# Trunk of mixed attention layers on one core: weight tiles seven and five, squares by pairs, rotary steps on VectorE, retention scores a unit later

## The chip, the cores and the metric

The kernel runs on one core of a Trainium2 chip. A core has TensorE (called PE in the profile; it multiplies matrices and loads its weights beside the multiplication, PEld), VectorE (DVE), ScalarE (ACT), GpSimd (POOL) and SyncE (SP), which issues most DMA transfers here. The engines run side by side and wait for one another through semaphores; each executes its own instructions in the order in which the program lists them. The metric is the time of one execution on the device in microseconds, the median over the runs; lower is better. One execution was also taken by the hardware profiler.

## The reference

The model is a decoder trunk of two layers on 256 tokens of width 1024, in float32, followed by a last RMSNorm. A layer is:

```python
for l in range(DEPTH):                      # DEPTH = 2
    h = rms_norm(x, attn_norm[l])
    p = h @ w_in[l]                         # 6560 columns
    cq, ckv, k_rope, mq, mk, mv, rq, rk, rv, rg, g_mla, g_moba, g_ret = split(p)
    o_mla  = causal attention over low-rank cq, ckv (normed, projected up) with rotary parts
    o_moba = block attention over mq, mk, mv; with 256 tokens one block: causal attention, partial rotary
    o_ret  = retention over rq, rk, rv in chunks of 128 with decay, group norm, times silu(rg)
    merged = sigmoid(g_mla) * (o_mla @ w_mla) + sigmoid(g_moba) * (o_moba @ w_moba) + sigmoid(g_ret) * (o_ret @ w_ret)
    x = x + merged @ w_out[l]
    h = rms_norm(x, mlp_norm[l])
    x = x + square(relu(h @ w_mlp_up[l])) @ w_mlp_down[l]
return rms_norm(x, final_norm)
```

Rotary embedding turns pairs of rows of a head: `x1*cos - x2*sin` and `x1*sin + x2*cos`. RMSNorm needs, for each token, the sum of the squares of its 1024 values.

## The kernel before

**Precision.** Products run as three TensorE products of split numbers: a value is held as a high part and a low part in a fast 32-bit format, and `high*high + low*high + high*low` is summed in PSUM (`three`, L221 to L223). In a turned projection (`project_turned`) the same three go as eight products over both parts of the activations (L378, 512 columns) and eight with the low part of the weights (L380, 256 columns).

**Weights.** All weights stream from memory once. A block of 128 x 1024 values is loaded by SP into a tile `raw` (`transfer`, a pool of RAW = 7 tiles); ScalarE copies it into its high part `whi` (L200), and VectorE subtracts to get its low part `wlo` (L202). There are six tiles of each; a block is loaded and split one unit ahead or more, and a tile comes free when the last matmul that reads it is done.

**Activations.** X holds the residual stream turned, 128 rows (channels) by 256 tokens in each of eight row chunks. `Normed` makes the operand of the products after a norm: for each chunk ScalarE writes the high part of x times the gain (L236) and VectorE the low part (L237), tiles `xs`. The factor 1/rms isn't in there; it is put in behind the products, from sums of squares that are made beside them. For that, `Normed.square(n)` (L266 to L273) squares a chunk on ScalarE (128x256) and adds it to `sqsum`; the addition runs on GpSimd or VectorE by the argument `on_pool`, and in this kernel on GpSimd. `Normed.stats` (L293) sums over the partitions with four small matmuls into `pss`, scales them on VectorE (L325), takes the power −1/2 on GpSimd (L326) and halves a copy on VectorE (L299). `stats_row` turns the result into a row by two transposes (L331), which ScalarE copies to `rrow` (L321). Layer 0's first norm takes its statistics from x by tokens instead and uses no `square`.

**Order of the work.** A layer is a list of units (`prog`): in layer 1 the low-rank projection b0, then mq (four units of turned projection), mk (four), mv, the gates gmla and gmoba of the branches, retention's rqk, rv and rg, the branch products, and so on; in layer 0 b0 and mq are made together in the start. Beside the units, steps are hung on places of the list by `at(slot(key, j), step)`: a step is emitted behind that unit. So `c_norms` (with squares and statistics in layer 1) follows unit 1 of mq, `stats_row` unit 2, `moba_rope` for mq follows the mk units 1 and 3 in layer 1, and for mk the units 1 and 3 of gmla0. The scores of retention (`ret_scores`, L444) follow unit 0 of rg. A scheduler that simulates the engines' times then fixes the order of each engine's instructions, over all that is emitted and with limits from the pools; a stretch at the layer change and the ends is in the written order on TensorE.

**Rotary of turned heads.** `project_turned` leaves pairs of heads in `qkraw` (L385 adds the two halves of an accumulator). `rope_turned` then loads a copy with the quarters swapped by four DMAs on SP (`qkoth`, L406), and makes `qkT = qkraw*cos + qkoth*sin` with one product L409, one product L410 and one sum L411, each over 128x512. For MoBA all three run on GpSimd, for retention L409 and L411 run on VectorE and L410 on GpSimd. The tables with cos and sin are multiplied by 1/rms on GpSimd (L397).

**Accumulators.** PSUM holds four accumulators `acc` of 512 columns and four for other uses. In layer 1, b0 holds two of `acc` until `c_norms` has read them.

The lines that the change touches are L196, L197 (the split tiles), L249 to L273 (`Normed`), L400 to L412 (`rope_turned`), L643 to L650 (`c_norms`), L720 to L723 (`moba_rope`), L823 (place of the mq rope), L887 (`ret_pair`), L998 (place of the scores) and L1219 (RAW).

## Time and profile before

| | |
|---|---|
| runs | 838.18, 837.26 and 837.96 us, median 837.96 |
| profiled execution | 838.08 us, of which 836.3 us span |
| TensorE clock granted | 0.998 in the mean |
| TensorE busy | 827.3 us, 99% of the span, 4382 instructions |
| VectorE busy | 587.7 us, 70% |
| ScalarE busy | 483.8 us, 58% |
| GpSimd busy | 92.7 us, 11%, 82 instructions |
| read from memory | 150.77 MB, 182 GB/s over the span |

The span runs from the first to the last instruction on the core; the time of an execution is 1.8 us longer. Rows of the profile name an engine, a line of the kernel, an operation and the tiles `out<-in`; a row of a timeline starts with its start and its length in us; rows of groups end with the summed busy time, the mean duration of one in ns, and the idle time ahead of them with what released it. The duration of a matmul in a row holds the latency of its pipeline: the next one starts well before it ends, 0.23 us after it for 512 columns, 0.12 us for 256.

### The profile page before, as it was taken

What the parts mean: (1) busy time and instruction counts of PE and PEld (TensorE: products, weight loads), DVE (VectorE), ACT (ScalarE), POOL (GpSimd) and SP (SyncE); (2) the same over time, 40 slices, a digit from 0 to 9 for tenths busy, and PEclk for the clock granted to TensorE, in tenths of its full rate; (3) what the DMA queues carried; (4) which work ended last, traced back from release to release, by engine and by line L of the source; (5) the groups of instructions that cost most, each with busy time, mean ns of one, the idle gap of its engine ahead of it and who ended that gap; (6) DMA issues with size and microseconds to landing.
All of it is one profiled execution on the core that took longest, in us unless ns stands there. A gap on an engine that the chain in (4) does not pass through costs nothing.

```text
span 836.3 us, 12164 instructions
## 1 busy us (share of the span) xinstructions
PE 827.3 (99%) x4382; PEld 702.6 (84%) x4382; DVE 587.7 (70%) x1069; ACT 483.8 (58%) x860; POOL 92.7 (11%) x82
## 2 busy tenths in 40 slices
PE   9999999999999999999999999999999999999997
PEld 7888878888888888888889887888888888888886
DVE  6987667595787666665699975766868775556663
ACT  7767665445556555555676575663555555555552
POOL 0321100040030000000037210002201200000000
PEclk9999999999999999999999999999999999999999
DMA  9966644646457656565465667456565656666611
GB/s 340 359 189 203 213 141 141 197 131 221 141 186 226 184 195 191 189 196 167 133 231 175 190 189 237 154 141 181 157 200 164 213 176 194 198 194 187 196 55 50
DMA packets 45324, 155.23 MB, mean 186 GB/s; under 512 B 5584, under 2 KB 6608, under 8 KB 45008
## 3 DMA queue, kind: packets, MB, share of 16 engines
q1 hardware_dynamic: 44688, 153.79, 58.4%
q8 instruction: 34, 0.56, 0.3%
q10 hardware_dynamic: 576, 0.67, 0.2%
q14 instruction: 26, 0.21, 0.1%
HBM read 150.77 MB, written 1.05 MB: 182 GB/s over the span
## 4 chain that ended last, share of the span: by engine, by line
PE 94%; DMA 2%; DVE 2%; SPq 1%; ACT 0%; POOL 0%; issue 0%; POOLq 0%; DVEq 0%
PE acc L221 17%; PE acc L223 17%; PE acc L222 17%; PE pup L1069 13%; PE pup L1071 7%; PE acc L1019 5%; PE acc L378 4%; PE acc L380 2%; PE ps_s L829 1%; PE ps_pt L478 1%; DMA raw<-wts 1%; DMA qkoth<-qkraw 1%; DVE wlo L202 1%; PE po L505 1%; PE ps_s L444 1%; SPq L406 1%
## 5 line engine op out<-in xcount | busy, mean ns | idle before, releaser
L202 DVE TENSOR_TENSOR wlo<-raw,whi 128x1024 fp32r<-128x1024 f32 (+4 forms) x287 | 343.6, 1204 | 183.2 <-ACT whi L200 130.0
L200 ACT ACTIVATE whi<-raw 128x1024 fp32r<-128x1024 f32 (+4 forms) x287 | 292.3, 1024 | 192.9 <-PE acc L223 115.2
L1069 PE MATMUL pup<-xs,whi 128*128 128x512 f32 x496 | 121.5, 390 | 0.0
L221 PE MATMUL acc<-whi,xs 128*128 128x512 f32 (+1 forms) x304 | 120.2, 395 | 0.0
L223 PE MATMUL acc<-whi,xs 128*128 128x512 f32 (+1 forms) x304 | 118.5, 391 | 0.4 <-DVE xs L237 0.4
L222 PE MATMUL acc<-wlo,xs 128*128 128x512 f32 (+1 forms) x304 | 118.8, 391 | 0.0
L1069 PEld LDWEIGHTS pup<-xs,whi 128*128 128x128 f32 x496 | 91.9, 188 | 18.3
L221 PE MATMUL acc<-whi,sq 128*128 128x512 f32 x256 | 100.1, 391 | 0.0
L222 PE MATMUL acc<-wlo,sq 128*128 128x512 f32 x256 | 99.9, 390 | 0.0
L223 PE MATMUL acc<-whi,sq 128*128 128x512 f32 x256 | 98.8, 389 | 0.0
L1071 PE MATMUL pup<-xs,wlo 128*128 128x256 f32 x496 | 68.8, 283 | 0.0
L1071 PEld LDWEIGHTS pup<-xs,wlo 128*128 128x128 f32 x496 | 65.7, 191 | 3.1
L223 PEld LDWEIGHTS acc<-whi,xs 128*128 128x128 f32 x304 | 57.1, 188 | 12.4 <-DVE xs L237 0.7
L221 PEld LDWEIGHTS acc<-whi,xs 128*128 128x128 f32 x304 | 57.1, 188 | 11.5 <-issue 0.7
L222 PEld LDWEIGHTS acc<-wlo,xs 128*128 128x128 f32 x304 | 57.2, 188 | 10.7
L1080 ACT ACTIVATE relu<-relu 128x256 f32<-128x256 f32 x64 | 25.6, 410 | 54.3 <-DVE relu L1079 54.3
L223 PEld LDWEIGHTS acc<-whi,sq 128*128 128x128 f32 x256 | 48.1, 188 | 10.2
L221 PEld LDWEIGHTS acc<-whi,sq 128*128 128x128 f32 x256 | 48.2, 188 | 9.2
L222 PEld LDWEIGHTS acc<-wlo,sq 128*128 128x128 f32 x256 | 48.2, 188 | 9.0
L273 POOL TENSOR_TENSOR sqsum<-sqsum,xsq 128x256 f32<-128x256 f32 x21 | 23.3, 1111 | 290.7 <-issue 172.4
L378 PE MATMUL acc<-xs,whi 128*128 128x512 f32 x160 | 41.3, 395 | 0.7 <-DVE qkraw L385 0.7
L467 ACT ACTIVATE prob<-prob,smx 128x128 f32<-128x128 f32 x64 | 28.4, 445 | 18.3 <-DVE smx L464 18.3
(243 smaller groups left out, 1153.4 us busy)
## 6 DMA issues: line engine op xcount, KB each, us to landing
raw<-wts SPq DMA_DIRECT2D x264, 512.0 KB, 4.2
raw<-wts SPq DMA_DIRECT2D x6, 464.0 KB, 8.5
qkoth<-qkraw SPq DMA_DIRECT2D x40, 64.0 KB, 4.5
dec<-consts SPq DMA_DIRECT2D x2, 1024.0 KB, 4.8
raw<-wts SPq DMA_DIRECT2D x4, 416.0 KB, 3.2
xrow<-xtok SPq DMA_DIRECT2D x4, 256.0 KB, 8.0
gn<-gn SPq DMA_DIRECT2D x2, 512.0 KB, 5.4
raw<-wts SPq DMA_DIRECT2D x3, 256.0 KB, 3.7
```

The costliest lines, as they stand in the source:

```text
L200: nc.scalar.activation(hi[:, cs], raw[:, cs], AF.Copy)
L202: nc.vector.tensor_sub(lo[:, cs], raw[:, cs], hi[:, cs].bitcast(F32))
L221: nc.tensor.matmul(o, ah, bh, start=start, stop=False)
L222: nc.tensor.matmul(o, ah, bl, start=False, stop=False)
L223: nc.tensor.matmul(o, al, bh, start=False, stop=stop)
L273: (nc.gpsimd if n < self.on_pool else nc.vector).tensor_add(self.sum, self.sum, sq)
L378: nc.tensor.matmul(acc, wh[:, k, :], xn.both(k), start=k == 0, stop=False)
L467: nc.scalar.activation(p[:, a:b], p[:, a:b], AF.Exp, bias=m[:, 2 + i : 3 + i], scale=scale, accum_out=m[:, 4 + i : 5 + i])
L1019: nc.tensor.matmul(o, a, b, start=half == 0 and i == 0, stop=4 * half + n == KD and i == len(jobs) - 1)
L1069: nc.tensor.matmul(u, w, xm.both(k), start=k == 0, stop=False)
L1071: nc.tensor.matmul(u[:, 0:S], w, xm.k(k)[0], start=False, stop=k == KD - 1)
L1080: nc.scalar.activation(s, s, AF.Square)
```

## The change

Five edits, which are one change:

- The split tiles `whi` and `wlo` get a constant SPLIT = 7 instead of six tiles each, and RAW goes from 7 to 5, so that the three pools hold 19 tiles in both cases.
- For the first norm of layer 1, `Normed.squares` takes the place of eight calls of `square`: ScalarE squares two row chunks at once (128x512) into a tile of the pool `w2k`, VectorE adds these four tiles (three sums of 128x512) and then the two halves (one of 128x256). The argument `on_pool` goes; the other norms that used `square` keep GpSimd for the sums.
- `rope_turned` runs all three operations on VectorE, for MoBA as for retention, in both layers.
- In layer 1 the rope of the mq pairs moves from the mk units 1 and 3 to the units 0 and 2 of gmla0.
- The scores of retention move from unit 0 of rg to unit 1.

```diff
-        hi = wp.tile([P, 1024], F32R, name="whi", bufs=6)
-        lo = wp.tile([P, 1024], F32R, name="wlo", bufs=6)
+        hi = wp.tile([P, 1024], F32R, name="whi", bufs=SPLIT)
+        lo = wp.tile([P, 1024], F32R, name="wlo", bufs=SPLIT)
...
-                (nc.gpsimd if n < self.on_pool else nc.vector).tensor_add(self.sum, self.sum, sq)
+                nc.gpsimd.tensor_add(self.sum, self.sum, sq)
+
+        def squares(self):
+
+            both = []
+            for n in range(0, KD, 2):
+                both.append(w2k("xsq2"))
+                nc.scalar.activation(halves(both[-1]), X[n // 4][:, n % 4 : n % 4 + 2, :], AF.Square)
+                if n:
+                    nc.vector.tensor_add(both[0], both[0], both[-1])
+            self.sum = sb.tile([P, S], F32, name="sqsum", bufs=1)
+            nc.vector.tensor_add(self.sum, both[0][:, 0:S], both[0][:, S : 2 * S])
...
-    def rope_turned(raw, tab, engine):
+    def rope_turned(raw, tab):
...
-        engine.tensor_mul(halves(o), halves(raw), cos)
-        nc.gpsimd.tensor_mul(halves(other), halves(other), sin)
-        engine.tensor_add(o, o, other)
+        nc.vector.tensor_mul(halves(o), halves(raw), cos)
+        nc.vector.tensor_mul(halves(other), halves(other), sin)
+        nc.vector.tensor_add(o, o, other)
...
             if l:
-                for n in range(KD):
-                    xn.square(n)
+                xn.squares()
                 xn.stats()
...
-                at(slot("mk", 1 + 2 * i), lambda i=i: moba_rope("mq", i))
+                at(slot("gmla0", 2 * i), lambda i=i: moba_rope("mq", i))
...
-        at(slot("rg", 0), lambda: in_a_row(ret_scores, moba_last))
+        at(slot("rg", 1), lambda: in_a_row(ret_scores, moba_last))
...
-RAW = 7
+RAW = 5
+SPLIT = 7
```

More of the change, by code (lines that the diff above doesn't have):

```diff
@@ L246, in trunk, with __init__ @@
     class Normed:
-        def __init__(self, g0, on_pool):
-            self.g0, self.on_pool = g0, on_pool
+        def __init__(self, g0):
+            self.g0 = g0
             self.parts = [t4(f"xs{i}").rearrange("p (k two) s -> p k two s", two=2) for i in range(KD // 2)]
@@ L594, in trunk @@
     nc.sync.dma_start(X[0][:, 1, :], x[:, 1, :])
-    xn = Normed(G_ATT, 0)
+    xn = Normed(G_ATT)
     xrows = [w2k("xrow") for _ in range(2 * NT)]
@@ L722, in moba_rope @@
                 mqkv["tab"] = tables(xn, TAB)
-            qkT[key][i] = rope_turned(mqkv[key, i], mqkv["tab"], nc.gpsimd)
+            qkT[key][i] = rope_turned(mqkv[key, i], mqkv["tab"])
         if l:
@@ L886, in ret_pair @@
                 rqkv["tab"] = tables(xn, rqkv["dec"][:, RT_H * 3 * P :])
-            rT.append(rope_turned(raw, rqkv["tab"], nc.vector))
+            rT.append(rope_turned(raw, rqkv["tab"]))
         rT, or_ps, aT, rg, oret = [], [], {}, {}, []
@@ L1033, in wout_first @@
         def wout_first():
-            xm.append(Normed(G_MLP + KD * l, KD))
+            xm.append(Normed(G_MLP + KD * l))
             some = [(load_w(l, "wout", n, 0), acc_tile()) for n in range(FIRST)]
@@ L1136, in layer @@
         if not last:
-            xn = Normed(G_ATT + KD * (l + 1), KD)
+            xn = Normed(G_ATT + KD * (l + 1))
             ys = {}
```

## The prediction

> **What bounds the kernel now.** I read the page's busy times first, then the chain that ended last, then TensorE's waits, and last the timeline around each wait.

> ```profile
> PE 827.3 (99%) x4382; PEld 702.6 (84%) x4382; DVE 587.7 (70%) x1069; ACT 483.8 (58%) x860; POOL 92.7 (11%) x82
> PE 94%; DMA 2%; DVE 2%; SPq 1%; ACT 0%; POOL 0%; issue 0%; POOLq 0%; DVEq 0%
> PE warm L616 <- PEq L1294: 0.8, 1, 0.8
> PE acc L378 <- DVE qkraw L385: 0.7, 1, 0.7
> PE b L705 <- ACT whi L200: 0.6, 1, 0.6
> PE ps_r L444 <- DVE qkT L411: 0.5, 1, 0.5
> PE acc L223 <- DVE xs L237: 0.4, 1, 0.4
> ```

> TensorE works for 827.3 of 836.3 us, and the last five rows are all its waits (total, times, longest). So the time moves only where a TensorE wait appears or goes. The matmuls are the same before and after, so I looked for waits alone: the three at L378, L444 and L223 lie at places the change touches, and the changed order of instructions is searched for new ones. The other two (start, first weights) are not touched in what they wait for. The gaps below are from start to start, less the usual spacing of 0.23 us (0.19 for 416 columns), and so 0.15 us larger than these rows.

> **Squares: the wait for xs L237 (the layer change).** Now VectorE and GpSimd work at once here.

> ```profile
> 416.13 1.13 DVE L237 SCALAR_TENSOR_TENSOR xs<-x,GX,xs 128x128 fp32r<-128x128 f32 x4
> 420.45 1.22 DVE L202 TENSOR_TENSOR wlo<-raw,whi 128x1024 fp32r<-128x1024 f32 x1
> 421.59 2.65 DVE L237 SCALAR_TENSOR_TENSOR xs<-GX,xs 128x128 fp32r<-128x128 f32 x4
> 424.16 2.23 DVE L237 SCALAR_TENSOR_TENSOR xs<-x,GX,xs 128x128 fp32r<-128x128 f32 x4
> 421.42 3.48 POOL L273 TENSOR_TENSOR sqsum<-sqsum,xsq 128x256 f32<-128x256 f32 x4 [172.37 <-issue]
> 421.73 0.34 PE L222 MATMUL acc<-wlo,xs 128*128 128x416 f32 x1
> 422.46 0.46 PE L223 MATMUL acc<-whi,xs 128*128 128x416 f32 x1 [0.39 <-DVE xs L237]
> ```

> Four xs take 1.13 us with GpSimd idle, 2.65 and 2.23 us while it adds squares. The gap is 422.46 − 421.73 − 0.19 = 0.54. In the changed order the squares come after all eight splits and GpSimd does none, so an xs takes about 0.33. In front of the first xs stands one longer split than now (1024 columns instead of 832, 0.2 us more). First xs 421.77 to 422.10, TensorE 422.15: gap 0.23, a gain of **0.31** (bounds: all 0.54; nothing, if the longer split eats it).

> [...]

> The squares themselves: eight of 128x256 become four of 128x512 on ScalarE, and VectorE gains three sums of 128x512 and one of 128x256. Prices: 0.69 and 0.42 us (rows of these sizes follow), 2.5 us on VectorE, no TensorE wait of its own. They take the cover from the next step, though.

> **Squares: the statistics one unit later.** Normed.stats (pss L293) now stands behind the second unit of mq in TensorE's order, in the changed order behind the fourth (mq,3).

> ```profile
> 432.31 0.50 PE L293 MATMUL pss<-ones,sqsum 128*128 128x1 f32 x4
> 433.54 2.11 PE L378 MATMUL acc<-xs,whi 128*128 128x512 f32 x8 [0.74 <-DVE qkraw L385]
> 435.50 1.11 PE L380 MATMUL acc<-xs,wlo 128*128 128x256 f32 x8
> 438.64 0.38 PE L331 MATMUL pss<-K,ms 128*128 128x128 f32 x2
> 430.81 2.35 DVE L202 TENSOR_TENSOR wlo<-raw,whi 128x1024 fp32r<-128x1024 f32 x2
> 433.08 0.41 DVE L385 TENSOR_TENSOR qkraw<-acc,second 128x256 f32<-128x256 f32 x1
> 434.55 0.15 DVE L325 TENSOR_SCALAR ms<-pss 128x2 f32<-128x2 f32 x1
> 435.51 0.17 DVE L299 TENSOR_SCALAR half<-ms 128x2 f32<-128x2 f32 x1 [0.49 <-POOL ms L326]
> 434.77 0.71 POOL L326 TENSOR_TENSOR ms<-ms,neghalf 128x2 f32<-128x2 f32 x1 [4.97 <-DVE ms L325]
> 438.68 1.05 ACT L200 ACTIVATE whi<-raw 128x1024 fp32r<-128x1024 f32 x1
> ```

> Today the pss matmuls at 432.31 are followed by two units (433.54 to 438.64) before anything needs the pow of L326; GpSimd's 0.71 us is covered. The two units before it also have a gap: mq,2 waits until 433.54 for the bank that qkraw L385 empties, which queues behind splits (0.88 us). Afterwards the same copy is still behind five splits, the last bound to the end of mq,0, while pss is gone from between: TensorE starts mq,2 at about 432.72 after ending mq,1 at 432.0, gap 0.72, a gain of **0.16** (bounds −0.2 to 0.4).

> At 2.9 us a unit (433.54 to 436.44 by the rows of L378 and L380), mq,2 and mq,3 then end at about 438.5. Right behind them stand pss, the row transposes L331 (which need the pow), and the first mk unit, whose accumulator the next qkraw L385 must empty; all four are in use, two by b0 until c_norms. On VectorE that copy is queued behind L325, L299 and a split whose slot comes free only at the end of mq,3. Step by step: end of mq,3 438.5, split 1.13 to 439.8 (a little under the 1.22 us above), L325 0.15 and the hop to GpSimd 0.08, L326 0.71, hop 0.03, L299 0.08 to the next start, L385 0.41 and hop 0.05: 441.3. TensorE's own work between is pss 0.37 and L331 0.22, to 438.9. A **new gap of 2.4**. If the split ran ahead of it, the chain from pss is 0.53 + 0.15 + 0.08 + 0.71 + 0.03 + 0.08 + 0.41 + 0.05 = 2.04, less the 0.6 of work: 1.4. Bounds 1.4 to 2.5; I take 2.4, since that split is in front in VectorE's order and waits on TensorE. Nothing on TensorE stands behind that could be drawn forward: its order is fixed.

> **Rotary steps on VectorE.** Ten products L410, six L409 and six sums L411 leave GpSimd.

> ```profile
> L410 POOL TENSOR_TENSOR qkoth<-qkoth,tab 128x512 f32<-128x512 f32 x10 | 15.1, 1506 | 163.5 <-DMA qkoth<-qkraw 149.4 <-PE ps_s L829 14.1
> L411 DVE TENSOR_TENSOR qkT<-qkT,qkoth 128x512 f32<-128x512 f32 x4 | 2.8, 693 | 13.2 <-POOL qkoth L410 13.2
> L385 DVE TENSOR_TENSOR qkraw<-acc,second 128x256 f32<-128x256 f32 x20 | 8.3, 416 | 0.0
> 450.00:500.00 50.00, 50.00 (x276) 42.43 (x275) 44.96 (x92) 31.93 (x63) 13.08 (x8) 1.00 0.61 183
> ```

> VectorE gets 22 × 0.69 = 15.2 us, where GpSimd needs 1.51 for one by the first row. In 450 to 500 VectorE is busy 44.96 of 50 us (third of the busy columns after the length, GpSimd's 13.08 the fifth). The stretch takes eight of the steps, 5.5 us, as its GpSimd count shows; what pays for it is that its other work runs free, as xs does above (1.13 against 2.65). I cost it at nothing; the cover is the weights split several us ahead. If that is gone, 44.96 + 5.5 is 0.5 over the 50 us before anything is released, and with softmax steps queued behind it I put the upper bound of this step at 2 us; the lower is nothing, since no wait of TensorE there names VectorE today. In layer 1 the qkoth loads of mq move from the mk units to the first gate: on SP twelve then stand together behind fifteen weight loads, still well before their L410. Nothing waits for them.

> **Scores one unit later (L444).**

> ```profile
> 566.51 1.30 POOL L410 TENSOR_TENSOR qkoth<-qkoth,tab 128x512 f32<-128x512 f32 x1 [12.51 <-DMA qkoth<-qkraw]
> 567.85 0.69 DVE L411 TENSOR_TENSOR qkT<-qkT,qkoth 128x512 f32<-128x512 f32 x1 [5.41 <-POOL qkoth L410]
> 567.82 0.39 PE L223 MATMUL acc<-whi,xs 128*128 128x512 f32 x1
> 568.68 1.58 PE L444 MATMUL ps_r<-qkT 64*128 64x256 f32 x16 [0.48 <-DVE qkT L411]
> ```

> The gap is 568.68 − 567.82 − 0.23 = 0.63. The scores move by 12 matmuls, 2.7 us, and L410 costs 0.69 instead of 1.30: **0.64 goes**. Next in line is ret_values, still two units behind the scores (5.5 us), so nothing new.

> **Seven split tiles, five raw.** The order of TensorE in layer 0 shifts with it: kvup's two pv groups now come first, and both KK groups behind.

> ```profile
> 53.70 0.28 PE L223 MATMUL acc<-cTh,wlo 128*128 128x256 f32 x1
> 56.03 0.49 PE L804 MATMUL pqr<-K,qr 128*128 128x128 f32 x3
> 56.28 0.47 PE L221 MATMUL acc<-whi,xs 128*128 128x512 f32 x1
> 54.02 0.68 DVE L774 COPY KK<-acc 64x512 f32<-64x512 f32 x1 [0.63 <-PE acc L223]
> 54.72 0.69 DVE L775 COPY KK<-acc 64x512 f32<-64x512 f32 x1
> ```

> The mv unit at 56.28 takes the accumulator that the first KK group filled until 53.70: 2.6 us lie between. After the change only the second group and pqr do: 7 × 0.12 + 0.25 = 1.1. The copies need 0.32 + 0.70 + 0.69 + 0.05 = 1.75 from that last start (54.02 − 53.70, then the two rows). A **new gap of 0.65** (bounds 0 and 0.9). The supply itself I cost at nothing: no row of TensorE's waits but the start names a split, so a seventh tile has nothing to win, and five raw tiles lose only where a load comes late: 0 to 1.

> **Sum.** −0.31 − 0.16 + 2.4 − 0.64 + 0.65 = +1.94 on the profiled 838.08 us (836.3 span and 1.8 around it): 840.0. That execution stands 0.12 over the median of 837.96, so **839.9**. All low ends give −0.54 − 0.4 + 1.4 − 0.64 + 0 = −0.2, all high ends +0.2 + 2.5 − 0.3 + 0.9 = +3.3: own range 837.8 to 841.3.

> **Rivals.** 0.2% of 837.96 is 1.7 us, about what a measurement can tell: 836.3 to 839.6 counts as the same.
> - The late statistics cost their low end and the KK copies nothing: −1.11 + 1.4 = +0.3, 838.3. For it: the split in front may get its slot earlier than I read. Against: it waits on the last matmul of mq,3.
> - Ending on the other side: VectorE reaches L325 with mq,3 still running, because TensorE keeps a unit in hand there, and no new gap appears. The removed gaps alone give −0.54 − 0.88 − 0.64 = −2.06: 835.9. It decides from where the new gaps together stay under 0.4 us. Against it: GpSimd's pow alone is 0.71 and now uncovered.
> - VectorE becomes the bound in 450 to 500, or a weight comes late behind the twelve qkoth loads: +2 on top, 841.9. For it: 90% busy. Against: no wait there today, and GpSimd's releases.
> - The change does nothing where it aims: the split tiles. That is my base case for them and contained in all sums.

> **Chances.** Forecast 0.54 (0.42 of it over 839.6, 0.12 under), the cheap case 0.22, the other side 0.12 (0.11 under 836.3), VectorE or queue 0.12 (0.10 slower). Faster 0.11, same 0.37, slower 0.52. Range 837.2 to 842.0: it leaves out the other side and a little above.

> **What would show it.** Right: in the waits of TensorE the rows L378 ← qkraw L385 grow to about 3 us in two places, or L331 ← ms L326 appears, near 439; L444 ← qkT and L223 ← xs go or shrink; a row of acc ← KK L775 near 56 of about 0.5. xs takes 1.1 to 1.3 for four. Wrong: no gap over 1 us between 436 and 442, or waits for whi or wlo in 450 to 500, or at the layer change for raw.

## The result, and the profile after

The changed kernel takes 840.53 us in the median of six executions (840.01 to 842.29); the kernel before, beside it, 837.38 us (837.10 to 838.18). The ratio is 1.0041, with a 95% interval of 1.0028 to 1.0054: slower by 0.4%, which is more than the 0.2% that the prediction took for the same. The forecast was 839.9 us, slower, in a range of 837.2 to 842.0.

The profiled execution is one of 842.29 us, span 840.5. TensorE's waits in it (total, times, longest) are:

```profile
PE pss L341 <- POOL ms L336: 2.0, 1, 2.0
PE acc L221 <- DVE KK L784: 0.8, 1, 0.8
PE warm L626 <- PEq L1304: 0.8, 1, 0.8
PE acc L388 <- DVE qkraw L395: 0.6, 1, 0.6
PE acc L388 <- ACT c L661: 0.2, 1, 0.2
```

Lines behind the change are numbered about ten higher: L388 was L378, L341 was L331, L336 was L326, L784 was L775, L395 was L385. Against the kernel before, the waits for qkT and for xs have left the list (a gap of 0.27 us is left at xs). The wait for the first weights is gone too; it belongs to the start, where executions of one kernel differ (0.6 and 0.3 us in two profiles of the kernel before). The first two rows are new, and they are the two that the prediction announced: the row transposes wait for GpSimd's power, and the mv unit of layer 0 for the KK copies.

The busy times, the line of section 1 of the page:

```profile
PE 830.0 (99%) x4382; PEld 704.2 (84%) x4382; DVE 589.0 (70%) x1095; ACT 483.2 (57%) x856; POOL 48.6 (6%) x53
```

GpSimd went from 92.7 us to 48.6, and VectorE took over 26 instructions more for 1.3 us more (587.7 to 589.0). TensorE was busy 2.7 us longer with the same 4382 instructions. The prediction had no place for that last number; the experiments on the gap explain most of it.

At the layer change, VectorE's timeline of the changed kernel (start, length, engine, line; the idle time before and its releaser in brackets):

```profile
421.54 1.22 DVE L202 TENSOR_TENSOR wlo<-raw,whi 128x1024 fp32r<-128x1024 f32 x1
422.67 1.14 DVE L237 SCALAR_TENSOR_TENSOR xs<-GX,xs 128x128 fp32r<-128x128 f32 x4
423.72 1.14 DVE L237 SCALAR_TENSOR_TENSOR xs<-x,GX,xs 128x128 fp32r<-128x128 f32 x4
439.79 1.23 DVE L202 TENSOR_TENSOR wlo<-raw,whi 128x1024 fp32r<-128x1024 f32 x1 [1.56 <-ACT whi L200]
440.93 0.15 DVE L335 TENSOR_SCALAR ms<-pss 128x2 f32<-128x2 f32 x1
441.89 0.17 DVE L309 TENSOR_SCALAR half<-ms 128x2 f32<-128x2 f32 x1 [0.81 <-POOL ms L336]
```

ScalarE's copy that the split at 439.79 waits for:

```profile
438.70 1.06 ACT L200 ACTIVATE whi<-raw 128x1024 fp32r<-128x1024 f32 x1 [1.47 <-PE acc L388]
```

TensorE around the statistics:

```profile
438.50 1.11 PE L390 MATMUL acc<-xs,wlo 128*128 128x256 f32 x8
439.45 0.50 PE L303 MATMUL pss<-ones,sqsum 128*128 128x1 f32 x4
441.92 0.43 PE L341 MATMUL pss<-K,ms 128*128 128x128 f32 x2 [1.96 <-POOL ms L336]
442.54 3.54 PE L388 MATMUL acc<-xs,whi 128*128 128x512 f32 x8 [0.19 <-ACT c L661]
```

Four xs take 1.14 us, where they took 2.65 and 2.23 beside GpSimd's sums. The price stands below: pss at 439.45 has nothing behind it on TensorE but the transposes, and those wait through ScalarE's copy of a weight block (438.70), the split of that block on VectorE (439.79), L335 and the power on GpSimd until 441.92. In the kernel before, 27 matmuls lay in this place. And the eight L388 of the next unit take 3.54 us, where eight took 2.0 to 2.1 us before.

In layer 0, VectorE's steps ahead of and at the KK copies, and the mv matmul that waits for them:

```profile
55.39 0.29 DVE L436 TENSOR_TENSOR qr<-ropea,ropeb 128x128 f32<-128x128 f32 x1
55.59 0.68 DVE L783 COPY KK<-acc 64x512 f32<-64x512 f32 x1
56.28 0.69 DVE L784 COPY KK<-acc 64x512 f32<-64x512 f32 x1
57.12 0.47 PE L221 MATMUL acc<-whi,xs 128*128 128x512 f32 x1 [0.80 <-DVE KK L784]
```

### The profile page after: what moved, and what is told of

It reads as the page before. It is cut to its first block, busy times and chain, and to the rows that moved or that the text cites. A ratio compares the mean times of both kernels' runs of the same rounds, so it can differ in the third digit from the quotient of the medians.

```text
span 840.5 us, 12137 instructions
## 1 busy us (share of the span) xinstructions
PE 830.0 (99%) x4382; PEld 704.2 (84%) x4382; DVE 589.0 (70%) x1095; ACT 483.2 (57%) x856; POOL 48.6 (6%) x53
## 3 DMA queue, kind: packets, MB, share of 16 engines
HBM read 150.77 MB, written 1.05 MB: 181 GB/s over the span
## 4 chain that ended last, share of the span: by engine, by line
PE 91%; DMA 4%; DVE 3%; issue 1%; ACT 1%; POOL 0%; SPq 0%; DVEq 0%; ACTq 0%; POOLq 0%
PE acc L221 17%; PE acc L223 17%; PE acc L222 17%; PE pup L1078 13%; PE pup L1080 7%; PE acc L1028 5%; PE acc L388 4%; DMA raw<-wts 2%; DVE wlo L202 2%; PE acc L390 1%; PE ps_pt L488 1%; PE ps_s L838 1%; DMA xrow<-xtok 1%; PE po L515 1%; PE ps_s L454 1%
## 5 line engine op out<-in xcount | busy, mean ns | idle before, releaser
L202 DVE TENSOR_TENSOR wlo<-raw,whi 128x1024 fp32r<-128x1024 f32 (+4 forms) x287 | 339.9, 1191 | 186.3 <-ACT whi L200 131.3
L200 ACT ACTIVATE whi<-raw 128x1024 fp32r<-128x1024 f32 (+4 forms) x287 | 292.2, 1023 | 188.8 <-PE acc L223 103.2
L221 PE MATMUL acc<-whi,xs 128*128 128x512 f32 (+1 forms) x304 | 119.6, 394 | 0.8 <-DVE KK L784 0.8
L223 PE MATMUL acc<-whi,xs 128*128 128x512 f32 (+1 forms) x304 | 119.8, 395 | 0.1
L222 PE MATMUL acc<-wlo,xs 128*128 128x512 f32 (+1 forms) x304 | 118.6, 390 | 0.0
L221 PE MATMUL acc<-whi,sq 128*128 128x512 f32 x256 | 100.2, 391 | 0.0
L222 PE MATMUL acc<-wlo,sq 128*128 128x512 f32 x256 | 100.0, 390 | 0.0
L223 PE MATMUL acc<-whi,sq 128*128 128x512 f32 x256 | 98.8, 389 | 0.0
L221 PEld LDWEIGHTS acc<-whi,xs 128*128 128x128 f32 x304 | 57.2, 188 | 12.5 <-PE pqr L813 1.0
L223 PEld LDWEIGHTS acc<-whi,xs 128*128 128x128 f32 x304 | 57.1, 188 | 11.9 <-DVE xs L237 0.5
L222 PEld LDWEIGHTS acc<-wlo,xs 128*128 128x128 f32 x304 | 57.2, 188 | 10.4
L223 PEld LDWEIGHTS acc<-whi,sq 128*128 128x128 f32 x256 | 48.1, 188 | 10.2
L221 PEld LDWEIGHTS acc<-whi,sq 128*128 128x128 f32 x256 | 48.2, 188 | 9.2
L222 PEld LDWEIGHTS acc<-wlo,sq 128*128 128x128 f32 x256 | 48.2, 188 | 8.9
L388 PE MATMUL acc<-xs,whi 128*128 128x512 f32 x160 | 43.0, 407 | 0.8 <-DVE qkraw L395 0.6
L388 PEld LDWEIGHTS acc<-xs,whi 128*128 128x128 f32 x160 | 29.9, 196 | 7.0 <-DVE qkraw L395 0.8
```

Of the source, the lines that this page charges most:

```text
L200: nc.scalar.activation(hi[:, cs], raw[:, cs], AF.Copy)
L202: nc.vector.tensor_sub(lo[:, cs], raw[:, cs], hi[:, cs].bitcast(F32))
L221: nc.tensor.matmul(o, ah, bh, start=start, stop=False)
L222: nc.tensor.matmul(o, ah, bl, start=False, stop=False)
L223: nc.tensor.matmul(o, al, bh, start=False, stop=stop)
L388: nc.tensor.matmul(acc, wh[:, k, :], xn.both(k), start=k == 0, stop=False)
```

## The experiments

The kernels are the changed one with an edit, unless the text says that the edit is made to the kernel before. Each was timed beside the kernel before on the same chip, whose medians were 837.62 us (beside no_squares, split_back, filled and early), 837.82 us (beside longer, raw5, only_squares and free_banks) and 837.35 us (beside only_rotary, only_scores and only_split).

| run | median us | ratio to before, 95% interval |
|---|---|---|
| changed kernel | 840.53 | 1.0041 (1.0028 to 1.0054) |
| no_squares | 838.33 | 1.0009 (1.0000 to 1.0018) |
| split_back | 839.74 | 1.0028 (1.0017 to 1.0038) |
| filled | 840.45 | 1.0033 (1.0021 to 1.0045) |
| longer | 843.45 | 1.0067 (1.0053 to 1.0081) |
| raw5 | 840.52 | 1.0031 (1.0020 to 1.0041) |
| only_squares (on before) | 840.29 | 1.0027 (1.0017 to 1.0038) |
| only_split (on before) | 838.98 | 1.0021 (1.0012 to 1.0029) |
| only_rotary (on before) | 837.35 | 0.9998 (0.9989 to 1.0007) |
| only_scores (on before) | 837.37 | 0.9999 (0.9990 to 1.0008) |
| early | 836.68 | 0.9989 (0.9980 to 0.9998) |
| free_banks | 836.02 | 0.9977 (0.9968 to 0.9987) |

**The squares taken back.**

```diff
-                xn.squares()
+                for n in range(KD):
+                    xn.square(n)
                 xn.stats()
```

> The changed kernel with the eight squares of 128x256 and GpSimd's sums back in c_norms; everything else stays changed. Theory A (most of the loss is the statistics behind mq,3): the wait of L341 for the pow, 2.0 us in the profile of the changed kernel, and the matmuls at 0.43 us behind it go; the waits for xs (0.5) and for L378 (0.9) are as before, the one of 0.96 for KK stays. 837.4 + 0.96 - 0.64 = 837.7, between 837.2 and 838.3. Theory B (VectorE has too much, or five raw tiles are too few): the rotary steps and pools are still changed, so at least half of the loss stays, 839 or more.

Measured: 838.33 us, 2.2 us less than the changed kernel. The wait for the power is gone, and those for xs, qkraw and KK are what is left:

```profile
PE warm L626 <- PEq L1305: 0.8, 1, 0.8
PE acc L388 <- DVE qkraw L395: 0.7, 1, 0.7
PE acc L223 <- DVE xs L237: 0.6, 1, 0.6
PE acc L221 <- DVE KK L785: 0.5, 1, 0.5
```

Theory A holds: most of the loss is the place of the statistics. The time is 0.03 us over the upper end that I gave; the 0.64 us that I took off for the scores are missing, of which more below.

**The squares alone.** The kernel before, with `xn.squares()` in c_norms.

> The kernel before with only the squares by pairs on VectorE inside c_norms. Theory A: this part alone places the statistics behind mq,3. The wait of L341 is 2.0 us, the one for xs halves, the one for qkraw and the one for the scores stay: 837.5 + 2.4 - 0.35 = 839.6 (839.0 to 840.2), some executions 1.9 us longer by the clock. Theory B (the loss needs the rotary steps on VectorE or the tile counts as well): under 838.5.

Measured: 840.29 us, 2.5 us over its neighbour and just above the expected range; in four of its seven executions the clock fell behind the gap, of which more below. The wait `PE pss L341 <- POOL ms L336` stands at 2.0 us. So this part alone moves the statistics behind mq,3, without the rotary steps and the tile counts. Theory B falls.

**The tile counts.**

```diff
-RAW = 5
-SPLIT = 7
+RAW = 7
+SPLIT = 6
```

> The changed kernel with six split tiles and seven raw tiles as before. Theory A: the tile counts matter only through the order of kvup in layer 0. KK's first group stands ahead of pv again, the wait L221 <- KK of 0.8 us goes, that of the statistics stays at 2.0: one us less than the changed kernel in executions of the same clock, 839.2. Theory B (raw tiles starve): more than 1.5 us less, 838.7 or under. If the wait for KK stays, my reading of its cause is wrong.

Measured: 839.74 us, 0.8 us less than the changed kernel; the KK wait has left the list, the power's 2.0 us stay. That is half a microsecond over the 839.2 that I expected. The clock explains it: three of the seven executions have a mean granted clock of 0.997 and took 840.38 to 840.84 us, the other four 0.999 and 839.45 to 839.74 us. Next, five raw tiles with six split ones, and the change of the counts alone on the kernel before:

> The changed kernel with six split tiles as before and five raw tiles as changed, so with two tiles less than either. Theory A: five raw tiles cost nothing; it is the seventh split tile that lets the planner draw pv ahead of the KK groups in layer 0. The same as with six and seven, 839.7 (839.3 to 840.2), no wait for KK. Theory B (with five raw tiles loads come late): waits for whi or raw appear, over 840.5; or the KK wait is back, and it was the raw tiles.

> The kernel before with only seven split and five raw tiles. Theory A: the order of kvup in layer 0 changes with the tiles alone; the wait of the mv unit for KK or for the copies behind it is back with 0.5 to 1.0 us, all else as before: 838.4 (838.0 to 838.9). Theory B (the tile counts alone do nothing; the order needs the rotary steps too): 837.7.

With five raw and six split tiles no KK wait is there, so with five raw tiles it is the seventh split tile that makes it. The median, 840.52 us, is over my bounds, but five raw tiles are not the reason. Six of the seven executions have a mean granted clock of 0.997 (840.45 to 841.17 us); the one at 0.999 took 839.43 us. At the same clock the times lie with those of split_back. The profiled execution is one with the clock lost: it was granted 0.72 from 439 to 442 us and 0.50 from 442 to 443. Its wait at the start (`PE b L714 <- ACT whi L200`, 0.4 us) left TensorE no later than in split_back: pss starts at 437.99 us here and at 438.51 there. The counts alone on the kernel before cost 1.6 us (838.98 against 837.35), slightly over my bounds; these rows of its TensorE timeline show the place in layer 0:

```profile
55.99 0.49 PE L814 MATMUL pqr<-K,qr 128*128 128x128 f32 x3
57.11 0.50 PE L221 MATMUL acc<-whi,xs 128*128 128x512 f32 x1 [0.63 <-ACT mv L687]
```

From the start of the last of the three pqr, 56.21, to the next matmul there are 0.9 us, of which 0.8 are a gap. The order of kvup is drawn together by the tile counts alone, as theory A said; which copy is last depends on the other parts (ScalarE's mv here, VectorE's KK in the changed kernel). The mv unit starts 0.8 us later than in the kernel before (57.11 against 56.28). Another 0.2 us lies at the layer change: two splits ahead of the xs take 2.35 us instead of 2.15, as one of them now has 1024 columns, and the wait for xs is 0.58 us instead of 0.39. Where the remaining half microsecond goes is not shown.

**Filling the gap, and lengthening it.** The eight slow L388 called for these two. The first puts matmuls of constants into the gap, the second makes it longer; both for the squares' statistics of layer 1 alone (the argument that limits them to it is left out of the diffs, and its value put in).

```diff
-            for t in range(NT):
-                nc.tensor.matmul(pt[:, t : t + 1], self.sum[:, P * t : P * t + P], ones[:, 0:1], start=True, stop=True)
+            with tc.manual_schedule(engines={mybir.EngineType.PE}):
+                for t in range(NT):
+                    nc.tensor.matmul(pt[:, t : t + 1], self.sum[:, P * t : P * t + P], ones[:, 0:1], start=True, stop=True)
+                pf = misc_tile("fill")
+                for i in range(8):
+                    nc.tensor.matmul(
+                        pf, nc.const_aps.tensor(1.0, [P, P], BF16), nc.const_aps.tensor(1.0, [P, 512], BF16), start=True, stop=True
+                    )
```

> The changed kernel with eight matmuls of constants (128x512, bf16) between the sums pss L303 and the transposes L341; they write a bank that nobody reads and leave the computation as it is. Theory C (the idle time of about 2 us lets TensorE's clock drop): the gap is now busy, L341 starts as late as before (the wait for the pow after the fillers is under 0.6 us), the matmuls behind it start every 0.23 us, the granted clock is 1.00 there and no execution stands at 842; median 840.1 (839.7 to 840.5), that is, of the two groups of executions only the lower one. Rival D (the matmuls at 0.43 us are slow for another reason, as the reads of X or of the accumulators by the other engines at that time): they stay at 0.43, and about a third of the executions stand near 842.

```diff
         nc.gpsimd.tensor_tensor(v[:, NT : 2 * NT], v[:, 0:NT], neghalf[:, 0:NT], op=ALU.pow)
+        for _ in range(2):
+            nc.gpsimd.tensor_tensor(v[:, NT : 2 * NT], v[:, NT : 2 * NT], ones[:, 0:NT], op=ALU.pow)
```

> The changed kernel with two further powers (exponent 1, which leaves the value) on GpSimd behind the pow of the late statistics, 0.7 us each: the gap ahead of L341 grows from 2.1 to 3.6 us. Theory C (idle time of TensorE lowers its clock, the longer the surer): 1.5 us more from the gap itself, and now most executions lose the 1.9 us of slow matmuls behind it too, where a third did: median 843.4 (842.6 to 844.2), granted clock under 0.7 behind the gap. Rival D (the slow matmuls have another cause): only the 1.5 us are added, two thirds of the executions at 841.7.

These rows are busy times by stretch (stretch, its length, TensorE, weight loads, VectorE, ScalarE, GpSimd with counts, then the granted TensorE clock, DMA share, GB/s). The changed kernel:

```profile
439.00:442.00 3.00, 1.04 (x11) 0.95 (x10) 1.40 (x4) 1.13 (x3) 0.69 (x1) 1.00 0.65 198
443.00:446.00 3.00, 3.00 (x9) 2.31 (x9) 2.90 (x15) 1.64 (x9) 1.55 (x3) 0.55 0.31 124
446.00:449.00 3.00, 3.00 (x20) 2.66 (x19) 1.79 (x4) 1.42 (x3) 1.32 (x2) 1.00 0.00 0
```

The run with the gap filled:

```profile
439.00:442.00 3.00, 2.81 (x18) 1.52 (x16) 1.58 (x4) 1.13 (x3) 0.70 (x1) 1.00 0.67 206
443.00:446.00 3.00, 3.00 (x19) 2.64 (x18) 2.97 (x15) 2.78 (x11) 1.50 (x3) 1.00 0.25 100
```

The run with the gap lengthened:

```profile
443.50:447.00 3.50, 3.50 (x10) 2.57 (x11) 3.43 (x16) 2.63 (x11) 1.45 (x2) 0.54 0.12 50
```

With the gap open, TensorE was granted 0.55 of its clock for the 3 us behind it and ran 9 instructions there; with the gap filled, 1.00 and 19. The wait for the power fell from 2.0 us to 0.2, though the transposes came as late as before. The six executions lie between 840.21 and 840.83 us, where two of the changed kernel's six were at 842.29 and 842.08 (mean granted clock 0.997) and four between 840.01 and 840.77 (0.999). With the longer gap all five lie between 843.17 and 844.57. Their median is 3.2 us over that of the changed kernel's four executions at 0.999 (840.23): 1.55 is what the gap grew by (3.65 less 2.10), and the other 1.7 I put down to the clock. The mean clock of each execution agrees: with the gap of 2.1 us open it is 0.997 in 15 of 27 (2 of 6 of the changed kernel, 3 of 7 of split_back, 6 of 7 of raw5, 4 of 7 of only_squares), with the longer gap 0.997 or less in all five, with the gap filled never under 0.998. Theory C holds for these runs and D falls: by its mean the clock was lost with an idle TensorE of 2.1 us in 15 of 27 executions, with 3.65 us in all five.

Why the same gap costs one execution and spares the next can be read from the clock. These rows are the changed kernel, then only_squares, whose profile kept its clock:

```profile
438.89:442.30 3.41, 1.45 (x13) 1.17 (x11) 1.70 (x4) 1.54 (x3) 0.69 (x1) 1.00 0.66 196
442.30:445.71 3.41, 3.22 (x9) 2.56 (x9) 3.34 (x17) 2.34 (x11) 1.51 (x2) 0.50 0.37 141
445.71:449.13 3.42, 3.42 (x22) 3.04 (x21) 2.14 (x8) 1.55 (x3) 1.36 (x2) 1.00 0.00 0
```

```profile
436.87:440.29 3.42, 2.09 (x16) 1.89 (x14) 1.76 (x4) 1.33 (x2) 0.11 (x1) 1.00 0.85 286
440.29:443.70 3.41, 2.58 (x13) 2.05 (x14) 2.72 (x11) 2.79 (x12) 1.92 (x3) 1.00 0.72 207
```

The half clock lasts 3.41 us in each of the three profiles that have it (changed kernel, raw5, longer). The trace's record of the clock consists, up to its last change, of stretches that are whole multiples of 3.413 us (128 steps up to the fall and 115 behind the half clock in these three profiles; 243 in split_back, only_squares and filled). So in these six profiles the clock changed on a grid of such steps, and the grid lay differently in the three that lost it: the record's first stretch starts 5.40 (changed kernel), 3.39 (raw5) and 6.38 us (longer) into the span. In the step ahead of the fall TensorE was busy for 1.45 us (changed kernel), 1.61 (raw5) and 0.02 (longer). In only_squares and split_back the same gap falls across the border of two steps, with 2.09 and 2.58 us busy in the one and 2.38 and 2.30 in the other, and the clock stays at 1.00; in filled the step has 3.03. In these six profiles, at this gap, a step with up to 1.61 us of work was followed by the half clock and one with 2.09 or more was not. From the 0.50 and the 3.41 us I estimate that a half clock takes up to 1.7 us of work, less where part of it lies in the gap.

**The rotary steps and the scores, each alone on the kernel before.**

> The kernel before with only the rotary steps changed: all 22 on VectorE, and mq's rope at gmla0 in layer 1. Theory A: VectorE's 15 us more lie beside TensorE and cost nothing, as its other work is freed of GpSimd; the scores' wait shrinks from 0.6 to 0 or stays: 837.4 (836.8 to 838.0). Theory B (VectorE becomes the bound between 450 and 500): waits of TensorE for probabilities, wlo or whi there, 838.5 or more.

> The kernel before with only the scores of retention one unit later. Theory A: the wait of L444 for qkT goes and nothing comes instead: 837.7 - 0.64 = 837.0 (836.6 to 837.4). Rival (the gap is given back at ret_values, two units behind): a new wait near 574, 837.7.

The rotary steps alone change nothing that these runs can tell: 837.35 us on both sides, with an interval from 0.9 us less to 0.6 us more. In the stretch where VectorE was busiest:

```profile
450.00:500.00 50.00, 50.00 (x272) 42.49 (x272) 42.32 (x96) 32.40 (x60) 0.00 (x0) 1.00 0.63 189
```

VectorE is busy 42.3 us of 50 there with 96 instructions, where it was busy 45.0 with 92 in the kernel before (44.2 with 93 in the second profile of it, named below): more instructions, and less time. Over the whole kernel VectorE's 1061 instructions other than the rotary products and sums took 568.5 us instead of 582.1 (580.6 in the second profile). The 13.08 us of GpSimd are gone from the stretch. That they had made VectorE's instructions longer is my reading of these numbers; in the first profile of the kernel before a split of 128x1024 (L202) took 1.99 us at 442.92, beside GpSimd's L409 (442.54 to 446.05), and 1.21 us at 433.41, with GpSimd idle. Not all of GpSimd's work does this: beside its L397 (440.13 to 442.58) a split took 1.22 us at 440.00.

The scores alone change nothing measurable either (837.37 against 837.35, interval 0.8 us less to 0.7 more), although the wait `PE ps_r L444 <- DVE qkT L411` is gone from that profile. So I took a second profile of the unchanged kernel before.

> The kernel before, unchanged, for a second profile. The run with only the scores moved lost its wait at L444 and no time. If the 0.64 us of the first profile belong to that execution alone (the load of qkoth landed late in it), this profile has no gap or one under 0.3 at L444 and a span of 835.6 or less; if they are there each time, the gap is 0.5 to 0.7 again, and the median of the moved scores stays unexplained. The gaps for xs (0.54) and qkraw (0.88) hang on the order alone and come again within 0.1.

Its waits, all of them:

```profile
PE warm L616 <- PEq L1294: 0.8, 1, 0.8
PE acc L378 <- DVE qkraw L385: 0.7, 1, 0.7
PE acc L223 <- DVE xs L237: 0.4, 1, 0.4
PE b L705 <- ACT whi L200: 0.3, 1, 0.3
```

The wait for the scores is not there. In GpSimd's timeline the product ahead of it begins earlier (first the second profile, then the first):

```profile
565.97 1.30 POOL L410 TENSOR_TENSOR qkoth<-qkoth,tab 128x512 f32<-128x512 f32 x1 [12.21 <-DMA qkoth<-qkraw]
```

```profile
566.51 1.30 POOL L410 TENSOR_TENSOR qkoth<-qkoth,tab 128x512 f32<-128x512 f32 x1 [12.51 <-DMA qkoth<-qkraw]
```

TensorE runs the same matmuls at nearly the same time in both; the load of qkoth landed half a microsecond later in the execution on which the forecast was built. The wait is not peculiar to that execution: the profile of only_squares, with the scores and GpSimd's product in the old place, has it again (0.4 us), and that of only_split, with both there too, has not. So two of four profiles have the wait. The gaps for xs and for qkraw are 0.54 and 0.88 us again, to the hundredth.

**A faster version.** If the statistics are late because VectorE's sums queue behind splits, the sums have to be listed earlier. The first step moves them to unit 3 of b0, with six split and seven raw tiles; the second also gives b0 in layer 1 two of the other four PSUM banks.

```diff
             project(l, "b0", xn, 416, b0.extend, before, ((0,), (1,)))
+            at(slot("b0", 3), lambda: xn.squares())
...
-                xn.squares()
                 xn.stats()
```

> The changed kernel with six split and seven raw tiles, and the squares hung on unit 3 of b0 instead of inside c_norms, so that VectorE's sums come ahead of the splits and the statistics behind mq,1 as in the kernel before. Theory A: neither the wait of 2.0 nor that of 0.8 is there, the one for the scores of retention is gone, the one for xs is half: 837.4 - 0.64 - 0.27 = 836.5 (836.0 to 837.2). Theory B (the load on VectorE costs time in itself): nothing gained against the kernel before, 837.4 or more. The wait for qkraw near 432 stays at 0.7 to 0.9.

```diff
-                accs.extend(acc_tile() for _ in range(NT))
+                accs.extend((tile_ or acc_tile)() for _ in range(NT))
...
-            project(l, "b0", xn, 416, b0.extend, before, ((0,), (1,)))
+            project(l, "b0", xn, 416, b0.extend, before, ((0,), (1,)), misc_tile)
```

> The kernel of the run named early, with the two accumulators of b0 in layer 1 taken from the other four PSUM banks, so that mq has all four of its own. The wait of mq,2 for qkraw near 432, 0.7 us, goes, since no unit needs the bank that the queued copy empties: 836.7 - 0.7 = 836.0 (835.6 to 836.6). If the statistics or the turn of c now wait for a bank instead, 836.7 or more.

Measured: 836.68 and 836.02 us, both within the bounds. The first number was partly luck: the expectation took off 0.64 us for the scores, which not every execution has, and only half of the gap for xs, all of which went. In the first, TensorE's timeline has pss at 431.09 and the transposes only at 435.02, with a unit of mq between:

```profile
431.09 0.50 PE L303 MATMUL pss<-ones,sqsum 128*128 128x1 f32 x4
435.02 0.38 PE L341 MATMUL pss<-K,ms 128*128 128x128 f32 x2
```

Both the gap for the power and that for xs are gone; the qkraw wait stays (0.5 us). In the second it goes too, and the whole list of TensorE's waits is one row, that of the start:

```profile
PE warm L626 <- PEq L1304: 0.8, 1, 0.8
```

Its ratio to the kernel before is 0.9977 (0.9968 to 0.9987): it beats the kernel before by 1.8 us (837.82 beside it), where the changed kernel lost 3.15 us to its own neighbour.

## Why the prediction was right

The direction and the mechanism came out; one term of the sum was not there, and one was missing. The size came out low: beside the kernel before, the change cost 3.15 us, and +1.94 was forecast. That 839.9 lies only 0.6 us from 840.53 is partly luck, since the kernel before ran at 837.38 there and not at the 837.96 on which the forecast stood. In the order of the steps:

- *xs beside GpSimd's sums.* Forecast gap 0.23, measured 0.27 (0.54 before). Four xs take 1.14 us, as the row without GpSimd said. The rest of the gap is the longer split, as forecast: in split_back and only_squares, with six split tiles, no gap is left.
- *mq,2 waits for qkraw.* Forecast 0.72, measured 0.80 (0.88 before).
- *The statistics behind mq,3.* Forecast gap 2.4 us. Measured 2.10 ahead of the transposes and 0.35 behind them: 2.45. The order was as worked out, with the split in front of L335 that I had put there, and this is the change's loss: the two runs on the squares give 2.2 and 2.5 us. That the size met so closely is luck. The working writes 439.8 where its steps give 439.6, and 438.9 where they give 439.1, so its own chain makes a gap of 2.05. What it lacked is ScalarE's copy of the block (438.70, 1.06 us), for which the split waits: it starts 0.34 us after TensorE has reached pss (439.79 against 439.45). And the mk unit was released by the copy of c (L661), not by qkraw.
- *KK in layer 0.* Forecast 0.65, measured 0.96 in this profile and 0.7 in those of no_squares, filled and longer, which have the same wait. The mv unit starts between 56.98 and 57.22 us in all four, against 56.28 before. I let the copies start 0.32 us after the last matmul of their group; VectorE was still at a rotary step (L436 at 55.39) and began at 55.59, 0.66 after it (54.93). I had named the tile counts as the cause; only_split shows it, and raw5 that it is the split tiles.
- *The rotary steps at nothing.* Right, within what the run can tell: 837.35 against 837.35. The rival in which VectorE becomes the bound between 450 and 500 falls: only_rotary has no TensorE wait there, and its VectorE is less busy there than before.
- *The scores, −0.64.* This term failed. The row that carried it was true of that execution; a second profile of the same kernel has no such gap, two of four profiles with the old place have it, and the edit alone moves the median by 0.02 us, though its interval reaches 0.8 us down. I had taken a wait that hangs on the landing of a DMA to be as fixed as one that hangs on an order.
- *What was missing: the clock.* I forecast the gap and took the work behind it at full speed. In two of the six executions TensorE lost about another 1.9 us there (840.2 to 842.1 us), of which 3.41 us at half the clock can take 1.7 by the estimate above. The median holds little of it, since four of six executions were spared; with 15 of 27 hit over the four kernels with this gap, that was luck.

With the second profile of the kernel before (837.52 us) as the start, the terms give −0.27 − 0.08 + 2.45 + 0.96 = +3.06, or 840.6; measured 840.53. So close a match is chance: two profiled executions of the kernel before lie 0.56 us apart (838.08 and 837.52). The rival in which no new gap appears needed VectorE to reach L325 with mq,3 still running; the profile has it at 440.93, 1.5 us after the end of mq,3. The rival with the statistics at their low end falls with the same row.

Two things stay open. The tile counts alone cost 1.6 us, of which the rows explain about 1.0. And the parts measured alone make 4.1 us (2.5 for the squares, 1.6 for the tiles) where the whole change costs 3.15. The clock is part of that: among executions that kept it, the squares alone cost 1.8 us (839.64 in the median) and the whole change 2.85 (840.23).

## What to carry to other kernels

When TensorE is full, read a change by where it puts small chains in TensorE's order: the sums cost 2.5 us on VectorE and nothing for that, and 2.45 us because the power behind them lost the two units that had covered it. Before a wait in a profile is booked as a gain, ask what ends it: two that end with an order of instructions came again to the hundredth in a second profile of the same kernel, and one that hangs on the landing of a DMA was there in two profiles of four. The gap of 2.1 us on TensorE was paid twice in 15 of 27 executions, the second time in the clock (0.997 in the mean), and in the profiles it went by where the gap fell in the clock's steps of 3.41 us; so either fill such a gap (granted clock 1.00 behind it) or move the work that needs it.

## What the runs showed of the hardware

Taking 22 operations on tiles of 128x512 from GpSimd to VectorE left VectorE's busy time over the whole kernel nearly as it was (587.7 and 586.2 us in two profiles of the kernel before, 589.0 in only_rotary), since its other 1061 instructions took 568.5 us instead of 582.1 and 580.6 without that work beside them on GpSimd.
